# Two settings of a two-block transformer kernel: four on-chip loads moved from ScalarE's queue to SyncE's, and no weight remainders on GpSimd

## The chip, the cores and the metric

One core of a Trainium2 chip. The metric is device time in microseconds of one execution, the median of several runs. TensorE (PE in the profile) multiplies, VectorE (DVE), ScalarE (ACT) and GpSimd (POOL) do the other arithmetic, and SyncE (SP) issues most loads. ACT and POOL can issue loads too: an issue takes its turn in the stream of the engine that makes it.

## What is computed

Two transformer blocks over 256 rows of width 1024, in fp32. The part of the first block that the change touches, cut down:

```python
def compress(kv, pos, w1, b1, w2, b2):
    r = kv.reshape(B, S // 16, 16, G, dk)
    blocks = jnp.concatenate([r[:, :-1], r[:, 1:]], axis=2) + pos
    h = jax.nn.gelu(jnp.einsum('bclgd,ldh->bcgh', blocks, w1) + b1)
    return jnp.einsum('bcgh,hd->bcgd', h, w2) + b2
...
def first_block(x, mem, ...):
    h = rms_norm(x, mix_norm_pre)
    q, kc, vc, ksl, vsl, kw, vw, gt, pin, u, v = jnp.split(h @ w_in, IN_SPLITS, axis=-1)
    out_a = nsa_mixer(...)      # compress(kc), compress(vc), then three softmaxes per head
    out_b = pool_mixer(pin, pool_w, pool_scale)
    out_c = sgu_mixer(u, v, ...)
    x = x + rms_norm(jnp.concatenate([out_a, out_b, out_c], -1) @ w_out, mix_norm_post)
    m = rms_norm(mem, mem_norm_kv)
    x = x + rms_norm(memory_attention(rms_norm(x, mem_norm_pre), m, w_mq, w_mk, w_mv, w_mo), mem_norm_post)
    return x + rms_norm(conv_ffn(rms_norm(x, ffn_norm_pre), ...), ffn_norm_post)
```

The second block follows (a gated delta rule, a sparse attention and a convolution side by side, a second memory attention, an MLP); the change does not touch its settings.

## The kernel before

**Products in three parts.** Each fp32 product is made of three matmuls of a reduced-precision form (`mm3`, L233 to L235): high part by high part, high part by low part and low part by high part. So each weight tile must be split when it arrives. `load_w` (L203 to L224) does this for a tile of 128 x 1024 (or 560) numbers: SP issues its load into `wr` (L208), ACT copies the rounded high part into `wh` (L221), and the DVE subtracts it to get the low part `wl`, in two halves (L223). `wr`, `wh` and `wl` have four buffers each, so a load waits until the weight four before it has been split, and a split until the matmuls of the weight four before it have run.

**Splits on POOL.** A share of the tiles is split in the other way: a counter `due` grows by `share` with each tile, and when it reaches 1 the tile goes through `split` with GpSimd, which makes the whole low part in one instruction (L229), with ACT's copy recorded at L228. `build` sets the share by stage through `give`: `G1` for the mixers of block 1, `GM` for its memory attention, and zero for all that follows. With the settings of before, seven tiles go to POOL: the third `w_in_a` tile and one of `w_out` under `G1`, five in the memory attention under `GM` (two of them of the second memory's key weight, loaded ahead into `bq` and its neighbours). A tile whose `wr` is the second memory's weight appears in the trace with the low part named `bq` or `gd_rhs`.

**Stages.** `block1_mix` makes the products of `w_in` by column chunks (`chunk_T`, 24 matmuls a tile, into `tp`), then those of `w_in_a` (values and gates, into `cc`), and then weaves two streams: `nsa` (the attention) and `fill1` (the two other mixers and, for the memory attention, the memory's norm, `w_mk` and `w_mv` products, into `fl`). After `w_out` come `residual` (norm of the result, added to x) and `block1_mem`.

**The compression.** The compressed keys and values are made in `a0` (named `a`, written by the DVE at L587) and shifted on the chip into `x2`, the second half of the buffer `qT`: for each of two groups one copy as it is (L592) and one shifted by a row into the other 64 partitions (L593). These four are loads from SBUF to SBUF, 128 KB each, and `T['xq']` names the engine that issues them. POOL adds the positions (`cmp_x`, L656, two halves for keys and two for values, in one buffer); TensorE multiplies by `cmp_w1` (L664, loads at L570); a short chain of DVE and ACT steps makes `hid` (gelu); then come L672, L681, and the first scores at L698. POOL also issues the bias table's loads into `bq` (L488) and computes the factor of every norm of rows (`rms_y`, L289) from `rms_v` (DVE, L287).

**Order.** The program is written stage by stage, but a scheduler places the instructions of each engine, by its own estimates, in one order, and each engine runs its own in that order. A change of two settings therefore moves many rows.

The lines on which the change bears:

```python
        for g in range(2):
            getattr(nc, T['xq']).dma_start(x2[0:64, :, g, :], kvc[g * 64:(g + 1) * 64, :, :])
            getattr(nc, T['xq']).dma_start(x2[64:128, :, g, :S - 1], kvc[g * 64:(g + 1) * 64, :, 1:])
...
        self.give(G1)
        x = self.block1_mix()
...
        self.give(GM)
        x = self.block1_mem(x)
```

Of the kernel before, what the change touches and what calls it, by code (L numbers as in the profile page):

```python
# [15 lines left out]
PSUM = bass.MemoryType.PSUM  # L16

FW0 = 1
R1, R2, DS, CV, CK, CV0, NW, FW, WARM, WARM2, G1, GM, GF, G2, GX, GP = 2.0, 2.5, 3, 0.5, 1, 0.25, 24, 14, 7, 4, 0.05, 0.2, 0, 0, 0, 0
T = dict(bp=0, bq='gpsimd', xq='scalar', cp=3, w=(2,3,7,8), n=32, hold=1)  # L20
P = 128
SCRATCH = 4096
S = 256
# [94 lines left out]
class Net:  # L118
# [348 lines left out]
    def build_bias(self):  # L467
# [11 lines left out]

        n, L = T['n'], 8 * 383 + 1  # L480
        copies = self.dp.tile([(n + 1) * L], F32, tag="tz", name="tz")
        rows = copies.rearrange("(p q) -> p q", q=L)[:n, :L - 1].rearrange("p (h u) -> h p u", h=8)
        getattr(nc, T['bq']).dma_start(rows, v[0:8, :383].unsqueeze(1).to_broadcast([8, n, 383]))
        self.biasB = self.t([P, 8, S], "bq8", bufs=1)
        for a in range(P // n):
            o = P - 1 - n * a
            diag = copies[o:o + n * (L - 1)].rearrange("(p q) -> p q", q=L - 1)
            getattr(nc, T['bq']).dma_start(self.biasB[a * n:(a + 1) * n], diag.rearrange("p (h u) -> p h u", u=383)[:, :, :S])  # L488

# [71 lines left out]
    def block1_mix(self):  # L561
# [6 lines left out]
        w1 = self.t([P, 4, 1024], "t3", bufs=1)  # L568
        tasks = [(T['bp'], self.build_bias), (T['cp'], self.more_constants)]
        tasks += [(T['w'][q], lambda q=q: nc.sync.dma_start(w1[:, q], self.i["cmp_w1"][q // 2, q % 2])) for q in range(4)]  # L570

# [19 lines left out]
# [3 lines that stand above are left out]
# [1214 lines left out]
```

## Time and profile before

| | |
|---|---|
| median of 3 runs | 873.55 us (872.27 to 873.56) |
| the profiled execution's own time | 878.08 us |
| its span | 876.3 us, 14992 instructions |
| mean granted TensorE clock | 0.98 of full speed |
| TensorE busy | 842.9 us (96% of the span) |
| VectorE busy | 615.7 us (70%) |
| ScalarE busy | 459.9 us (52%) |
| GpSimd busy | 88.9 us (10%) |
| HBM | 136 MB read, 157 GB/s over the span |

The span is the time from the first to the last instruction of one execution; the execution's own time holds what lies around it, 1.8 us. The profiled execution was 4.5 us longer than the median of the runs without a profile. "Idle before" in a row is the time for which its engine had nothing running just ahead of it, with the instruction that let it go on.

### The profile page before, as it was taken

The numbers are of one execution on the slowest core, as the hardware profiler recorded it, in microseconds if no ns is written. First come the engines' busy times: TensorE is split into PE (matmuls) and PEld (weight loads), VectorE is DVE, ScalarE is ACT, GpSimd is POOL, SyncE is SP. The second block draws the span as 40 slices with busy tenths as digits, with TensorE's granted clock in tenths as the row PEclk, the third lists the DMA queues.
The fourth block names the chain that finished last, engine by engine and source line by source line (L and its number), as shares of the span: only waits on it lengthen the run. The fifth ranks groups of instructions, "written<-read, shape, count | busy, mean of one in ns | idle before, by whom it ended". The sixth has DMA issues, their size and how long they took to land.

```text
span 876.3 us, 14992 instructions
## 1 busy us (share of the span) xinstructions
PE 842.9 (96%) x5725; PEld 768.1 (88%) x5725; DVE 615.7 (70%) x1333; ACT 459.9 (52%) x795; POOL 88.9 (10%) x119
## 2 busy tenths in 40 slices
PE   8899999998999999999999999899899999999998
PEld 6898977878887999999997998879898999999996
DVE  5568765555557878876776797989677776666663
ACT  5246454555655666655555764556456544444442
POOL 1224101121110000000001002520100000000000
PEclk9979999999999999999999998999999999999999
DMA  8985323477343666665652652201163366666661
GB/s 258 293 267 167 98 76 100 149 230 234 128 130 135 208 206 212 218 202 184 190 147 73 197 188 73 82 15 48 50 178 112 97 208 184 188 189 190 182 188 67
DMA packets 41012, 138.94 MB, mean 159 GB/s; under 512 B 4851, under 2 KB 6292, under 8 KB 40940
## 3 DMA queue, kind: packets, MB, share of 16 engines
q1 hardware_dynamic: 37440, 130.49, 47.7%
q10 hardware_dynamic: 2988, 6.06, 2.1%
q0 software_dynamic: 512, 1.44, 1.0%
q8 instruction: 45, 0.74, 0.3%
q14 instruction: 27, 0.22, 0.1%
HBM read 136.00 MB, written 1.44 MB: 157 GB/s over the span
## 4 chain that ended last, share of the span: by engine, by line
PE 79%; DVE 10%; DMA 4%; ACT 3%; issue 2%; POOL 2%; ACTq 0%; SPq 0%; POOLq 0%; DVEq 0%
PE tp L235 10%; PE tp L233 10%; PE tp L234 10%; PE fl L233 6%; PE fl L234 6%; PE fl L235 6%; PE cc L235 5%; PE cc L234 5%; PE cc L233 5%; DVE wl L223 2%; PE cc L751 1%; DVE cv_y L1522 1%; DMA srow<-in_srows_dram 1%; PE tp L729 1%; PE tp L919 1%
## 5 line engine op out<-in xcount | busy, mean ns | idle before, releaser
L223 DVE TENSOR_TENSOR wl<-wr,wh 128x512 fp32r<-128x512 f32 (+2 forms) x448 | 301.3, 698 | 118.7 <-ACT wh L221 116.7
L221 ACT ACTIVATE wh<-wr 128x1024 fp32r<-128x1024 f32 (+2 forms) x224 | 233.0, 1044 | 214.3 <-PE tp L234 80.7
L233 PE MATMUL tp<-thi,wh 128*128 128x256 f32 x784 | 222.7, 284 | 2.0 <-ACT wh L221 2.0
L235 PE MATMUL tp<-thi,wl 128*128 128x256 f32 x784 | 222.7, 284 | 0.2 <-DVE wl L223 0.2
L234 PE MATMUL tp<-tlo,wh 128*128 128x256 f32 x784 | 222.4, 284 | 0.0
L233 PEld LDWEIGHTS tp<-thi,wh 128*128 128x128 f32 x784 | 150.5, 192 | 3.6 <-ACT wh L221 2.2
L234 PEld LDWEIGHTS tp<-tlo,wh 128*128 128x128 f32 x784 | 150.5, 192 | 1.3
L235 PEld LDWEIGHTS tp<-thi,wl 128*128 128x128 f32 x784 | 150.5, 192 | 0.4 <-DVE wl L223 0.4
L228 ACT ACTIVATE ff_h<-ff_y 128x256 fp32r<-128x256 f32 x54 | 22.2, 416 | 42.9 <-PE fl L235 42.0
L233 PE MATMUL fl<-thi,wh 128*128 128x256 f32 x144 | 42.8, 297 | 1.5 <-ACT wh L221 1.4
L235 PE MATMUL cc<-wh,ff_h 128*128 128x512 f32 x108 | 42.4, 393 | 0.0
L973 DVE SCALAR_TENSOR_TENSOR ff_y<-tp,col,ff_y 128x255 f32<-128x255 f32 x88 | 41.9, 476 | 0.7 <-ACT ff_y L971 0.6
L233 PE MATMUL cc<-wh,ff_h 128*128 128x512 f32 x108 | 42.4, 392 | 0.0
L234 PE MATMUL cc<-wl,ff_h 128*128 128x512 f32 x108 | 42.2, 391 | 0.0
L234 PE MATMUL fl<-wl,ff_h 128*128 128x512 f32 x108 | 42.2, 391 | 0.0
L234 PE MATMUL fl<-tlo,wh 128*128 128x256 f32 x144 | 42.1, 292 | 0.0
L233 PE MATMUL fl<-wh,ff_h 128*128 128x512 f32 x108 | 42.1, 390 | 0.0
L235 PE MATMUL fl<-wh,ff_h 128*128 128x512 f32 x108 | 42.1, 391 | 0.0
L235 PE MATMUL fl<-thi,wl 128*128 128x256 f32 x144 | 42.0, 291 | 0.0
L289 POOL TENSOR_TENSOR rms_y<-rms_v,mhalf 128x1 f32<-128x1 f32 x16 | 9.8, 614 | 268.4 <-DVE rms_v L287 268.4
L229 DVE TENSOR_TENSOR ff_h<-ff_y,ff_h 128x256 fp32r<-128x256 f32 x54 | 22.5, 422 | 14.5 <-ACT ff_h L228 14.4
L233 PEld LDWEIGHTS fl<-thi,wh 128*128 128x128 f32 x144 | 28.4, 197 | 2.1 <-ACT wh L221 1.6
(495 smaller groups left out, 1763.2 us busy)
## 6 DMA issues: line engine op xcount, KB each, us to landing
wr<-in_mlp_w_dram SPq DMA_DIRECT2D x64, 512.0 KB, 3.6
wr<-in_w_up_dram SPq DMA_DIRECT2D x44, 512.0 KB, 3.6
wr<-in_w_in_dram SPq DMA_DIRECT2D x31, 512.0 KB, 4.6
wr<-in_w_down_dram SPq DMA_DIRECT2D x22, 512.0 KB, 3.6
wr<-in_w_out_dram SPq DMA_DIRECT2D x16, 512.0 KB, 3.6
grow<-in_rows_dram ACTq DMA_DIRECT2D x8, 512.0 KB, 5.3
wr<-in_w_mk_dram SPq DMA_DIRECT2D x8, 512.0 KB, 4.3
wr<-in_w_mv_dram SPq DMA_DIRECT2D x8, 512.0 KB, 3.5
```

The costliest lines, as they stand in the source:

```text
L221: nc.scalar.activation(hi, raw, AF.Copy)
L223: nc.vector.tensor_tensor(lo[:, q], raw[:, q], hi[:, q].bitcast(F32), op=ALU.subtract)
L228: nc.scalar.activation(hi, raw, AF.Copy)
L229: (eng or nc.vector).tensor_tensor(lo, raw, hi.bitcast(F32), op=ALU.subtract)
L233: nc.tensor.matmul(out, a[0], b[0], start=first, stop=False)
L234: nc.tensor.matmul(out, a[0], b[1], start=False, stop=False)
L235: nc.tensor.matmul(out, a[1], b[0], start=False, stop=last)
L289: self.nc.gpsimd.tensor_tensor(y, v, self.mhalf[:, :1], op=ALU.pow)
L729: nc.tensor.matmul(pc[:, :2 * ns], qT[:, j, tsl], kT[:, :, br, :ns], start=True, stop=True)
L751: nc.tensor.matmul(out[:, h * 64:(h + 1) * 64], pT[:, (e * (i + 1) + b) * P:(e * (i + 1) + b + 1) * P], vsw[b][:, vo:vo + 64], start=(b == ...
L919: nc.tensor.matmul(pc[:, o:o + P], v[b][:, c * P:(c + 1) * P], pT[:, (2 * e + b) * P:(2 * e + b + 1) * P], start=(b == 0), stop=(b == 1))
L973: nc.vector.scalar_tensor_tensor(y[:, e, k:], a[:, :S - k], self.c("conv_w", 44 * (2 - k) + c), y[:, e, k:], op0=ALU.mult, op1=ALU.add)
```

## The change

Two lines of settings:

```diff
-R1, R2, DS, CV, CK, CV0, NW, FW, WARM, WARM2, G1, GM, GF, G2, GX, GP = 2.0, 2.5, 3, 0.5, 1, 0.25, 24, 14, 7, 4, 0.05, 0.2, 0, 0, 0, 0
-T = dict(bp=0, bq='gpsimd', xq='scalar', cp=3, w=(2,3,7,8), n=32, hold=1)
+R1, R2, DS, CV, CK, CV0, NW, FW, WARM, WARM2, G1, GM, GF, G2, GX, GP = 2.0, 2.5, 3, 0.5, 1, 0.25, 24, 14, 7, 4, 0, 0, 0, 0, 0, 0
+T = dict(bp=0, bq='gpsimd', xq='sync', cp=3, w=(2,3,7,8), n=32, hold=1)
```

`xq='sync'` makes SP issue L592 and L593. `G1 = GM = 0` sends all seven tiles through the other branch of `load_w`: ACT's copy at L221 and two DVE halves at L223 instead of one POOL instruction.

On SP, around the loads of the compression (the difference; `wr` are weights, `t` is `cmp_w1`, `a` the source and `qT` the target of the four loads):

```order
 L208 DMA wr_421<-in_w_in_dram 128x1024
 L208 DMA wr_452<-in_w_in_dram 128x1024
+L592 DMA qT_344<-a_54_342 64x2x256
+L593 DMA qT_344<-a_54_342 64x2x255
+L592 DMA qT_344<-a_54_342 64x2x256
+L593 DMA qT_344<-a_54_342 64x2x255
 L208 DMA wr_490<-in_w_in_a_dram 128x560
 L208 DMA wr_509<-in_w_in_a_dram 128x560
-L570 DMA t_36_247<-in_cmp_w_dram 128x1024 x2
 L208 DMA wr_528<-in_w_in_a_dram 128x560
```

The four loads now stand behind two `w_in` weights and ahead of the first two `w_in_a` tiles; two `cmp_w1` loads moved further down.

On POOL, in the compression, before (`wl_531` is the low part of the third `w_in_a` tile; `cmp_x_581` and `cmp_x_675` are the keys' and the values' inputs):

```order
L656 TENSOR_TENSOR cmp_x_581<-qT_344,col 128x512
L488 DMA bq_40_259<-tz 32x8x256 x4
L229 TENSOR_TENSOR wl_531<-wr_528,wh_530 128x560
L656 TENSOR_TENSOR cmp_x_581<-qT_344,col 128x512
...
L656 TENSOR_TENSOR cmp_x_675<-qT_344,col 128x512 x2
L850 TENSOR_TENSOR wsT_767<-wsT_767,con 128x512
L289 TENSOR_TENSOR rms_y_969<-rms_v_967,mhalf 128x1
```

The same place on POOL now:

```order
L656 TENSOR_TENSOR cmp_x_582<-qT_344,col 128x512
L488 DMA bq_40_259<-tz 32x8x256 x4
L656 TENSOR_TENSOR cmp_x_582<-qT_344,col 128x512
...
L289 TENSOR_TENSOR rms_y_970<-rms_v_968,mhalf 128x1
L275 MEMSET rms_ss_1925 128x1
...
L656 TENSOR_TENSOR cmp_x_676<-qT_344,col 128x512 x2
```

The split is gone, and the factor of the memory's first norm (`rms_y_969`, now `rms_y_970`) has moved from behind the values' `cmp_x` pair to ahead of it. On TensorE the `L664` products of that pair stood ahead of the 48 products of `w_in_b`, and now stand behind them and behind ten of the next chunk (`fl_840`), some 58 matmuls later.

On the DVE, at the end of the attention, before (`oa` is the sum of the attention's three branches, `tlo` the low part of its transpose):

```order
L744 COPY pT_1664<-tp_1650 128x512
L765 TENSOR_TENSOR oat_1674<-cc_1517,cf_1670 128x512
L767 TENSOR_TENSOR oa_1291<-oa_1291,oat_1674 128x512
L302 TENSOR_TENSOR tlo_246<-tp_1677,thi_245 128x4x128
L223 TENSOR_TENSOR wl_1789<-wr_1786,wh_1788 128x512 x2
```

The same place on the DVE now:

```order
L744 COPY pT_1665<-tp_1651 128x512
L223 TENSOR_TENSOR wl_1772<-wr_1769,wh_1771 128x512
L765 TENSOR_TENSOR oat_1675<-cc_1518,cf_1671 128x512
L223 TENSOR_TENSOR wl_1772<-wr_1769,wh_1771 128x512
L767 TENSOR_TENSOR oa_1292<-oa_1292,oat_1675 128x512
L223 TENSOR_TENSOR wl_1791<-wr_1788,wh_1790 128x512 x2
L302 TENSOR_TENSOR tlo_246<-tp_1678,thi_245 128x4x128
```

The two halves of the split that POOL made stand on either side of L765, and two halves of the next weight ahead of L302.

## Rows read from the trace of the kernel before

**Rows 1.** The page: parts 1 (engines) and 5 (one group).

```profile
PE 842.9 (96%) x5725; PEld 768.1 (88%) x5725; DVE 615.7 (70%) x1333; ACT 459.9 (52%) x795; POOL 88.9 (10%) x119
...
L223 DVE TENSOR_TENSOR wl<-wr,wh 128x512 fp32r<-128x512 f32 (+2 forms) x448 | 301.3, 698 | 118.7 <-ACT wh L221 116.7
```

**Rows 2.** Busy time by stretch; PEclk, DMA share, GB/s last.

```profile
30.00:35.00 5.00, 3.14 (x14) 2.94 (x15) 3.38 (x7) 3.12 (x4) 0.00 (x0) 0.70 1.08 319
...
45.00:50.00 5.00, 5.00 (x27) 5.00 (x27) 1.82 (x3) 1.06 (x1) 0.03 (x1) 0.57 1.01 231
```

**Rows 3.** Timeline of PE: start, length, line, xcount, [idle before].

```profile
31.64 0.39 PE L233 MATMUL tp<-thi,wh 128*128 128x256 f32 x1 [1.96 <-ACT wh L221]
...
44.25 0.38 PE L233 MATMUL fl<-thi,wh 128*128 128x256 f32 x1 [1.41 <-ACT wh L221]
```

**Rows 4.** Timeline of ACT, 12 to 48 us (ACTq: DMA issues).

```profile
27.74 0.71 ACTq L592 DMA_DIRECT2D qT<-a  x1
...
30.53 3.12 ACT L221 ACTIVATE wh<-wr 128x1024 fp32r<-128x1024 f32 x4 [3.54 <-issue]
```

**Rows 5.** Timeline of SP, 20 to 60 us (SPq: DMA issues).

```profile
22.90 1.90 SPq L208 DMA_DIRECT2D wr<-in_w_in_dram  x2
```

**Rows 6.** Issues in 22.85:24, 27.7:30.5, 35.8:36.3, 61.5:62: KB, us to landing.

```profile
wr<-in_w_in_dram SPq DMA_DIRECT2D x1, 512.0 KB, 6.5
...
qT<-a ACTq DMA_DIRECT2D x2, 127.5 KB, 7.6
...
wr<-in_w_in_dram SPq DMA_DIRECT2D x1, 512.0 KB, 6.8
...
wr<-in_w_mk_dram SPq DMA_DIRECT2D x1, 512.0 KB, 4.7
```

**Rows 7.** The chain that ended last, 0 to 130 us: single steps.

```profile
27.02 0.69 DVE a L587
...
34.87 0.21 PE tp L233
...
37.09 0.12 PE tp L234
```

**Rows 8.** Timeline of POOL, 0 to 70 us.

```profile
37.79 1.14 POOL L656 TENSOR_TENSOR cmp_x<-qT,col 128x512 f32<-128x512 f32 x1 [22.04 <-DMA wr<-in_w_in_a_dram]
...
38.88 2.33 POOL L488 DMA_DIRECT2D bq<-tz  x4
...
66.24 0.58 POOL L289 TENSOR_TENSOR rms_y<-rms_v,mhalf 128x1 f32<-128x1 f32 x1 [8.57 <-DVE rms_v L287]
```

**Rows 9.** Timeline of PE, 52 to 74 us: the compression.

```profile
59.62 4.02 PE L664 MATMUL tp<-cmp_x,t 128*128 128x30 f32 x32
...
70.48 0.30 PE L672 MATMUL tp<-hid,w 128*128 128x30 f32 x2
...
71.91 1.03 PE L698 MATMUL tp<-kcT,qT 128*128 128x32 f32 x8
```

**Rows 10.** Timeline of POOL, 130 to 300 us.

```profile
142.36 2.38 POOL L229 TENSOR_TENSOR wl<-wr,wh 128x1024 fp32r<-128x1024 f32 x1 [3.06 <-issue]
...
173.57 3.07 POOL L229 TENSOR_TENSOR wl<-wr,wh 128x1024 fp32r<-128x1024 f32 x1 [3.00 <-ACT wh L228]
...
207.17 2.41 POOL L229 TENSOR_TENSOR bq<-wr,t 128x1024 fp32r<-128x1024 f32 x1 [2.01 <-ACT t L228]
```

**Rows 11.** Timeline of DVE, 138 to 180 us.

```profile
143.55 1.73 DVE L767 TENSOR_TENSOR oa<-oa,oat 128x512 f32<-128x512 f32 x1
...
175.17 0.15 DVE L287 TENSOR_REDUCE rms_v<-rms_ss 128x1 f32<-128x3 f32 x1
```

**Rows 12.** Timeline of PE, three of its waits.

```profile
145.43 0.63 PE L311 MATMUL tp<-con,oa 128*128 128x128 f32 x4 [0.96 <-DVE oa L767]
...
181.35 0.66 PE L311 MATMUL tp<-con,xh 128*128 128x128 f32 x4 [1.94 <-DVE xh L334]
...
220.03 3.96 PE L937 MATMUL tp<-memk,big 128*128 128x256 f32 x10 [4.20 <-ACT big L932]
```

## Prediction, on record before the changed kernel was run

> **What bounds the kernel now.** I read the page first: TensorE is busy 96% of the span, the DVE 70%, POOL 10% [rows 1]. So time can come only from the few places where TensorE waits or runs at its lower clock; the reader should look for those in the change's stages, not at the busy shares. Then the stretches: from 30 to 50 us the DMA engines are full (share 1.08 and 1.01) and TensorE's granted clock is 0.70 and 0.57 of full speed [rows 2]. Then TensorE's own rows: in that stage it waits twice for the high parts of a weight, 1.96 us until 31.64 and 1.41 us until 44.25 [rows 3]. Outside it, three waits stand near splits that the change takes off POOL: 0.96 us at 145.43, 1.94 us at 181.35, 4.20 us at 220.03 [rows 12]. All of this is under 12 us of 873.55.
>
> **Four loads from ScalarE to SyncE.** ACT's four x2 issues run from 27.74; only then, at 30.53, does its copy of the high parts begin, and that row gives "issue" as the reason for its idle time [rows 4]. The weight it copies was issued at 22.90 [rows 5] and took 6.5 us [rows 6]: there at 29.4. TensorE ran out of work at 31.64 − 1.96 = 29.68.
>
> Term a: with ACT free the copy starts at 29.4 instead of 30.53, 1.1 us sooner, and the wait falls from 1.96 to 0.87. I take −1.1. Bounds: 0 (the second weight behind it comes late as before) and −1.96.
>
> Term b: after that wait a single matmul takes 0.21 us, later 0.12 [rows 7]: the lower of the two clock levels, 1.2 against 2.4 GHz. The trace has waits of about 1 us after which the clock stayed, the one at 145.43 among them, and the one of 1.96 after which it fell. A wait of 0.87 should leave it up: 12 matmuls × 0.09 = −1.1; the bounds are that and 0.
>
> SyncE takes the issues instead. Their source is ready at 27.02 + 0.69 = 27.71 [rows 7], so ACT was not late with its first one at 27.74, and SP cannot be sooner. In SP's order they stand behind two weight loads (22.90 to 24.8 [rows 5]) and ahead of the first two w_in_a tiles, which had gone out while `a` was still being made. So SP now idles to 27.7, issues the four for 2.7 us as ACT did (0.71 and less each [rows 4]), and the two tiles and a cmp_w1 load go out after 30.4. Two things follow. The x2 transfers find the DMA engines emptier: they took 7.6 us [rows 6]; I take half of that for the last, so POOL, which waited for them to 37.79, starts some 3.6 us sooner, and with it the bias loads bq that it issues from 38.88 [rows 8]. And w_in_a comes later: a 512 KB load took 4.7 us where the engines were less full and 6.5 to 6.8 in this stage [rows 6], so it lands between 35.1 and 37.2. TensorE has 48 products of the two weights at hand, from about 30.5 at 0.12 [rows 7], which is 36.3. I cost this at nothing; that work hides it, and if the cover is gone it is up to 1.9 us (37.2 + 1.0 for copy and low part, less 36.3), which stands in the range.
>
> Term c: the wait at 44.25 is for a weight that was issued within 35.8 to 36.3 and took 6.8 us [rows 6], landing at 42.7. The bq loads now go 3.6 us sooner and take their share beside it; I give half of that to its delay: 44.6 with the rest of a microsecond for SP's later turn. Its copy takes about 1.0 (four in a row, two of them of half width, took 3.12 [rows 4]): 45.7. TensorE was there at 44.25 − 1.41 = 42.84; it is 2.2 us ahead, at 40.6, but the order now puts 22 products of w_in_a (0.13 each, 2.9) and half a compression stream (1 to 2 us, by rows 9 a stretch of 32 in 4.02) before it: 45.0. The wait falls from 1.41 to 0.7: −0.7. Bounds −1.41 and +2.3 (the load at about 48).
>
> Here a rule speaks against the change. The rows show that ACT's time is freed; they do not show that any transfer lands sooner. The Trainium skill, "DMA: Bandwidth & Descriptors", section "Issuing engines are not separate DMA queues", says that loads run on the same 16 DMA engines whoever starts them, and that another issuer saves the sequencer's time alone. The trace agrees in the full share of 1.08. By the rule taken strictly only a and b would stand; that is the first rival.
>
> Term d: from 45.7 to 52.5 the clock is at its lower level (0.57 in the stretch from 45 to 50) [rows 2]. It follows the 1.41 wait. 22 matmuls of the w_in_a product would run there, of 280 columns, so 0.23 against 0.13 by the pitches 0.21 and 0.12 for 256: −2.2. With even chances a new, shorter fall comes (14 × 0.09 = 1.3, half of it 0.65): −1.55. Bounds −2.2 and 0.
>
> Term e, a loss: the order puts the end of the compression later, with less work between its steps. cmp_x has one buffer; POOL needs 1.14 us for a half [rows 8], TensorE has 6 matmuls, 0.7 us, between: +0.45. From L672 to L698 took 71.91 − 70.48 = 1.43 us [rows 9]; now 5 matmuls (0.6) cover it: +0.8. From there to L681 I allow another 0.5. Together +1.8. Bounds 0 (other work covers it) and the price of the second rival.
>
> **No low parts on POOL.** Seven splits leave POOL: 1.40 to 3.07 us each there. A wide one becomes two DVE instructions of 0.70 us [rows 1]: 6 × 1.4 + 0.8 = 9.2 us more on the DVE, which is busy 615.7 us and has 30% of the span free. Where the DVE is ahead of TensorE this costs nothing; what hides it is a split that is done some tiles before its use. If that cover is gone, up to 9.2.
>
> Term f: the w_out split on POOL runs from 142.36 for 2.38 us [rows 10]; beside it the DVE's L767 takes 1.73 us [rows 11] where a 128x512 step takes 0.70 [rows 1], and TensorE waits 0.96 us for it [rows 12]. With POOL silent it loses 1.0 us, while one half of the split now stands between L765 and L767 (+0.7) and five matmuls (0.6) are put into the gap. I take −0.9; bounds −0.96 and +0.3.
>
> Term g: POOL computes the norm's rms_y. Its input is there at 175.17 + 0.15 = 175.32, but POOL is in a split from 173.57 to 176.64 [rows 10, 11]: 1.3 us late. The wait at 181.35 hangs on this norm. Half a split on the DVE stands ahead of the xh step, 0.7: net −0.6, and half a chance that the fall of the clock at 182 goes with the shorter wait, −0.7. Together −1.3; bounds −2.0 and +0.7.
>
> Term h: the same pattern at 207.17, where POOL is in a split for 2.41 us and the norm follows. The wait of 4.20 at 220.03 ends with work behind that norm [rows 10, 12]. I take −0.9, between 0 and −1.7, since other loads lie between.
>
> Term i: in the memory attention's softmax the split halves now stand between the DVE's short steps: two halves of 0.70 on a chain that TensorE waits for, less what lies beside other work: +1.0; bounds 0 and +2.1.
>
> Sum: −1.1 − 1.1 − 0.7 − 1.55 + 1.8 − 0.9 − 1.3 − 0.9 + 1.0 = −4.75. By the profiled execution's own time that is 878.08 − 4.75 = 873.3; it stands 4.5 us (0.5%) above the median of the runs, 873.55, so the prediction is the median less 4.75: 868.8.
>
> **Rivals.** A, no change: the loads are bound by the full DMA engines, and the earlier bq pushes the weight of term c to about 48 us. Then c is +2.3 and d is 0; the sum is −4.75 + 3.0 + 1.55 = −0.2, 873.4. For it: share 1.08 in the stage. Against it: the x2 loads take their 0.5 MB out of the stage sooner, and the total to be moved is the same. Chance 0.20.
>
> B, slower: one mechanism on POOL. In the new order the memory's rms_y stands ahead of the second pair of cmp_x steps, and ACT's copy of the first w_mk weight stands ahead of the square that this norm needs. TensorE's second compression stream began at 59.62 [rows 9]; it now stands some 58 matmuls later in its order (7 us), less the 4 us won, so about 62.5. If the memory's loads come as before, the first w_mk (issued about 61.6, 4.7 us [rows 6]) lands at 66.3; then copy 1.06, square 0.8, the norm 0.15 + 0.58, cmp_x 1.14 [rows 4, 8]: 70.0. TensorE waits 7.5 us and a fall of the clock adds 1.3. In place of e: −4.75 − 1.8 + 8.8 = +2.25, 875.8. It decides if that load lands after 59 us (62.5 less the 3.7 of that chain). For it: before, the norm's rms_y came at 66.24 [rows 8]. Against it: TensorE leaves the w_in_a weights 3 to 5 us sooner, so their buffers, and the loads behind them, come sooner too. Chance 0.17.
>
> C, better: e is covered, both new falls of the clock stay away, i is hidden: −4.75 − 1.8 − 0.65 − 0.7 − 1.0 = −8.9, 864.65. Chance 0.15.
>
> That the change does not do what it says can be left out: the orders show the issues on SP and no split on POOL.
>
> **How the numbers follow.** The forecast has 0.48, A 0.20, B 0.17, C 0.15. Under 0.2% (1.75 us) a measurement of this kernel cannot tell a time from no change. Faster takes the forecast, C and a sliver of A: 0.64; same is the rest of A: 0.19; slower is B: 0.17. The range reaches from C, less its own 0.6, to A and the milder part of B: 864.0 to 874.5. The forecast's own range is 866.5 to 871.5.
>
> **What would show it.** Right: in the profile after, ACT's copy near 29.4 with no "issue" idle, no lower clock from 32 to 35, a wait under 1 us near 45, L767 at 0.7 us, rms_y within 0.3 us of its rms_v. Wrong: a wait of several microseconds of TensorE for POOL's cmp_x between 60 and 70 us (B); the weight after the w_in_a product landing at 47 or later with a low clock behind it (A); waits for wl with the DVE as the one that ends them in the memory attention, beyond 2 us in all (then i was too small).

## The result, and the profile after

The changed kernel took 882.8 us (median of 4 runs, 881.87 to 885.95) against 873.31 us of the kernel before beside it: 1.0107 times as long, 95% interval 1.0076 to 1.0139. That is 9.5 us **slower**, where 4.75 us faster had been forecast. Its profiled execution took 881.97 us, near its own median; the one of before was 4.5 us above its median, so the two traces differ by less (3.9 us of span) than the medians. The clock tells why: TensorE's mean granted clock was 0.980 in that execution of before, and its median is 0.986 (0.981 to 0.990) in the runs of the same kernel beside the experiments. An estimate from this: 0.006 of 876 us, so the trace of before has some 5 us more of lost clock than a usual run.

The page of the changed kernel, parts 1 and 5:

```profile
PE 843.7 (96%) x5725; PEld 768.6 (87%) x5725; DVE 620.7 (71%) x1347; ACT 461.0 (52%) x795; POOL 73.8 (8%) x112
...
L223 DVE TENSOR_TENSOR wl<-wr,wh 128x512 fp32r<-128x512 f32 (+2 forms) x460 | 307.9, 695 | 133.5 <-ACT wh L221 131.7
```

Against [rows 1] POOL has lost 15 us of work, the DVE has gained 5, and TensorE's share is the same 96%: the page hides the loss. The stretches show it (same columns as [rows 2]):

```profile
30.00:35.00 5.00, 5.00 (x42) 5.00 (x43) 2.84 (x6) 2.17 (x3) 1.53 (x2) 1.00 1.04 311
...
45.00:50.00 5.00, 2.77 (x11) 2.55 (x12) 1.41 (x3) 2.27 (x3) 0.00 (x0) 0.61 0.99 294
60.00:65.00 5.00, 2.32 (x19) 2.12 (x18) 1.95 (x5) 3.38 (x8) 0.68 (x4) 1.00 0.29 100
65.00:70.00 5.00, 5.00 (x32) 4.82 (x31) 3.62 (x18) 0.71 (x4) 2.81 (x5) 0.66 0.94 314
70.00:75.00 5.00, 5.00 (x26) 5.00 (x25) 0.60 (x4) 0.82 (x1) 1.04 (x1) 0.50 0.00 0
75.00:80.00 5.00, 5.00 (x25) 5.00 (x25) 3.96 (x14) 1.59 (x4) 3.20 (x4) 0.50 0.06 25
```

From 30 to 35 us the loss of before is gone (clock 1.00, TensorE busy throughout). From 45 to 50 nothing is won: TensorE works 2.77 us, and the clock is still low. From 60 to 65 TensorE works 2.32 of 5 us, and from 70 to 80 it is busy all the time at the lower of its two levels, 0.50. TensorE's timeline tells what it does there:

```profile
29.25 0.39 PE L233 MATMUL tp<-thi,wh 128*128 128x256 f32 x1 [0.15 <-ACT wh L221]
...
42.09 1.87 PE L664 MATMUL tp<-cmp_x,t 128*128 128x30 f32 x16
47.23 0.58 PE L233 MATMUL fl<-thi,wh 128*128 128x256 f32 x1 [3.27 <-ACT wh L221]
...
64.43 0.38 PE L233 MATMUL fl<-thi,wh 128*128 128x256 f32 x1 [2.68 <-ACT sg_v L857]
...
68.33 7.03 PE L664 MATMUL tp<-cmp_x,t 128*128 128x30 f32 x32
...
79.59 1.29 PE L698 MATMUL tp<-kcT,qT 128*128 128x32 f32 x8
...
188.69 1.32 PE L311 MATMUL tp<-con,xh 128*128 128x128 f32 x8 [1.05 <-DVE xh L334]
...
225.59 4.97 PE L937 MATMUL tp<-memk,big 128*128 128x256 f32 x14 [3.82 <-ACT big L932]
```

The waits of [rows 3] went from 1.96 to 0.15 us and from 1.41 to 3.27 us; a new one of 2.68 us stands at 64.43. The values' stream of L664, which took 4.02 us for 32 records in [rows 9], takes 7.03. (A record is one row of the trace; each L664 instruction leaves two.) The transposition that began at 181.35 in [rows 12] begins at 188.69, 7.3 us later. By then TensorE has waited 3.1 us more in all (14.2 against 11.0), and has had 20.5 us at the lower level (6.8 from 46.1, 13.7 from 66.6) against 13.7 us before; half of the 6.8 us between them is lost: 3.4 us. Over the whole span the two traces have the same time at the lower level (35 us), since before has falls behind 181 us that are not there now. In the runs of the changed kernel the mean granted clock is 0.982, against the 0.986 of before; on 880 us the 0.004 is 3.5 of the 9.5 us. The rest would be waiting, of which the traces show 3.0 us; the other 3 us are not shown.

What TensorE waits for at 64.43 is the evacuation of the w_in_b products (`sg_v`, L857), which must leave the accumulator banks `fl` before the next products can go into them. ScalarE, timeline:

```profile
58.26 0.63 ACT L837 ACTIVATE sg_u<-sg_u 128x512 f32<-128x512 f32 x1
...
61.59 1.06 ACT L221 ACTIVATE wh<-wr 128x1024 fp32r<-128x1024 f32 x1 [2.09 <-DMA wr<-in_w_mk_dram]
...
63.92 0.46 ACT L857 ACTIVATE sg_v<-fl,rt 128x256 f32<-128x256 f32 x1
64.06 0.35 ACTq L818 DMA_DIRECT2D pl_c<-in_invcnt_dram  x1
64.28 0.46 ACT L857 ACTIVATE sg_v<-fl,rt 128x256 f32<-128x256 f32 x1
```

The copy of the first `w_mk` weight at 61.59 waited 2.09 us for its load; two squares follow, and only then comes `sg_v`, though its products were done at 61.75. GpSimd, timeline, and the wait's other side, the DMA issues of 28.4 to 28.6 and 35.4 to 35.6:

```profile
33.47 1.14 POOL L656 TENSOR_TENSOR cmp_x<-qT,col 128x512 f32<-128x512 f32 x1 [19.17 <-DMA qT<-a]
34.55 2.32 POOL L488 DMA_DIRECT2D bq<-tz  x4
...
64.12 0.57 POOL L289 TENSOR_TENSOR rms_y<-rms_v,mhalf 128x1 f32<-128x1 f32 x1 [24.32 <-DVE rms_v L287]
...
67.15 2.20 POOL L656 TENSOR_TENSOR cmp_x<-qT,col 128x512 f32<-128x512 f32 x2 [2.34 <-PE tp L664]
```

```profile
qT<-a SPq DMA_DIRECT2D x1, 127.5 KB, 4.8
...
wr<-in_w_in_dram SPq DMA_DIRECT2D x1, 512.0 KB, 10.6
```

The x2 loads land in 4.8 us instead of 7.6 [rows 6] and POOL starts 4.3 us earlier than at 37.79 [rows 8], bq too (1.3 of the 4.3 because the first x2 load goes out at 26.44 and not at 27.74); the weight that TensorE waits for to 47.23 now takes 10.6 us instead of 6.8.

### The profile page after: what moved, and what is told of

It reads as the page before. It is cut to its first block, busy times and chain, and to the rows that moved or that the text cites. A ratio compares the mean times of both kernels' runs of the same rounds, so it can differ in the third digit from the quotient of the medians.

```text
span 880.2 us, 15013 instructions
## 1 busy us (share of the span) xinstructions
PE 843.7 (96%) x5725; PEld 768.6 (87%) x5725; DVE 620.7 (71%) x1347; ACT 461.0 (52%) x795; POOL 73.8 (8%) x112
## 3 DMA queue, kind: packets, MB, share of 16 engines
q0 software_dynamic: 512, 1.44, 0.9%
HBM read 136.00 MB, written 1.44 MB: 156 GB/s over the span
## 5 line engine op out<-in xcount | busy, mean ns | idle before, releaser
L223 DVE TENSOR_TENSOR wl<-wr,wh 128x512 fp32r<-128x512 f32 (+2 forms) x460 | 307.9, 695 | 133.5 <-ACT wh L221 131.7
L221 ACT ACTIVATE wh<-wr 128x1024 fp32r<-128x1024 f32 (+2 forms) x230 | 239.4, 1043 | 226.5 <-PE tp L234 79.1
L234 PE MATMUL fl<-tlo,wh 128*128 128x256 f32 x144 | 44.2, 307 | 0.0
L235 PE MATMUL fl<-thi,wl 128*128 128x256 f32 x144 | 43.9, 305 | 0.0
L235 PE MATMUL cc<-wh,ff_h 128*128 128x512 f32 x108 | 42.4, 393 | 0.0
L233 PE MATMUL cc<-wh,ff_h 128*128 128x512 f32 x108 | 42.4, 392 | 0.0
L233 PEld LDWEIGHTS fl<-thi,wh 128*128 128x128 f32 x144 | 30.3, 211 | 6.5 <-ACT wh L221 3.4
```

What stands on the lines that cost most here:

```text
L221: nc.scalar.activation(hi, raw, AF.Copy)
L223: nc.vector.tensor_tensor(lo[:, q], raw[:, q], hi[:, q].bitcast(F32), op=ALU.subtract)
L233: nc.tensor.matmul(out, a[0], b[0], start=first, stop=False)
L234: nc.tensor.matmul(out, a[0], b[1], start=False, stop=False)
L235: nc.tensor.matmul(out, a[1], b[0], start=False, stop=last)
```

## The experiments

Theory: the loss is the late place of the compression. L664 comes in three runs (16 records for the first half of the keys, 16 for the second, 32 for the values). Before, 22 and 46 other products stood between them; now 100 and 6, so that the last 48 records come late and close together. Rivals: the DVE's 14 more halves cost as such, or SyncE's issues do. Times are medians, ratios are to the kernel before run beside. Where an edit adds lines, the lines behind it have numbers a little higher (L664 is L665 to L668 there).

**One part at a time.**

```diff
-xq='scalar'
+xq='sync'          (e1)
-G1, GM = 0.05, 0.2
+G1, GM = 0, 0.2    (e2)
+G1, GM = 0.05, 0   (e3)
```

> Only the four x2 loads go to SyncE; the shares G1 and GM stay 0.05 and 0.2. In the built order both compression streams (L664) again stand behind the w_in_b products and inside the next chunk, as in the changed kernel. Theory (late compression order is the loss): 879 to 885 us, with a lower-clock stretch of 7 us or more around the L664 products after 60 us. Rival 1 (the DVE's 14 extra halves are the loss): 872 to 874, since they are not here. Rival 2 (SyncE's issues and the earlier bq push the weight loads): 879 or more, with the loss before 50 us.

> Only G1 is 0; the x2 loads stay on ScalarE, GM stays 0.2. Two splits less on GpSimd, in the first block's mixers. In the built order the second half of the keys' stream and the values' stream stand behind w_in_b. Theory (late compression order): 879 to 885 us. Rival 1 (DVE halves): 874 to 876, two sevenths of the loss. Rival 2 (SyncE's issues): 872 to 874, since SyncE issues what it did.

> Only GM is 0; the order of the first 100 us is that of before. Theory (late compression order): 871 to 873.5 us, no loss, perhaps 1 to 2 us won where rms_y no longer stands behind a split on GpSimd. Rival 1 (DVE halves are the loss): 879 to 881, five sevenths of the loss. Rival 2: 873.

> The run with GM = 0 alone once more, with more rounds, beside the two above: 870 to 872 us, 0.1 to 0.5% under the kernel before.

e1: 887.67 us, 1.0176 (1.0146 to 1.0206). e2: 883.71 us, 1.0134 (1.0115 to 1.0154). e3: 871.26 us, 0.9970 (0.9944 to 0.9995), and in its second series 870.91 us, 0.9970 (0.9948 to 0.9992). So xq alone costs more than the whole change, G1 alone cannot be told from it (the intervals overlap), and the third part, GM, is a gain of 0.3%. That fits the theory: e1 and e2 both build the late place, e3 the early one; e1 is slower than the theory's 879 to 885. In e2 the DVE has only two splits more, in e3 five; the rival of the DVE's halves is out. In e2 SyncE issues what it did, so its issues are not needed for the loss either. e1's trace by stretch:

```profile
60.00:65.00 5.00, 5.00 (x45) 5.00 (x44) 1.44 (x3) 2.40 (x5) 0.00 (x0) 0.99 0.58 190
65.00:70.00 5.00, 4.77 (x32) 4.48 (x31) 3.87 (x12) 0.00 (x0) 3.17 (x3) 0.70 0.69 234
70.00:75.00 5.00, 5.00 (x25) 5.00 (x25) 0.25 (x3) 1.79 (x4) 0.08 (x1) 0.50 0.00 0
```

and its TensorE timeline there:

```profile
63.03 3.66 PE L664 MATMUL tp<-cmp_x,t 128*128 128x30 f32 x32
...
68.01 7.03 PE L664 MATMUL tp<-cmp_x,t 128*128 128x30 f32 x32 [0.23 <-POOL cmp_x L656]
```

Here no wait over 0.25 us comes between 56.7 and 84: the clock falls at 67.0, between the two L664 runs, while TensorE is busy, and stays down for 13.7 us. In e2 TensorE waits 5.89 us until 58.24 for the evacuation of the chunk before (`sg_u`, L836), and runs the last 32 records in 6.10 us:

```profile
58.24 0.58 PE L233 MATMUL fl<-wh,thi 128*128 128x256 f32 x1 [5.89 <-DVE sg_u L836]
```

**The place itself.** e5 keeps both edits and restores the early place; e6 keeps neither and makes it late; e7 puts the keys' stream early, the values' late; e8 is e5 with the x2 loads on ScalarE.

```diff
+with self.tc.high_priority(2000):                      (e5, e8; e7: 2000 if s == 0 else 0)
     nc.gpsimd.tensor_tensor(xa[:, half]..., op=ALU.add)     # L656
...
+with self.tc.high_priority(-130 if q and not s else 0):   (e6, on the kernel before)
     nc.tensor.matmul(pc[...], raw[...], rhs, ...)           # L664
```

> Both edits as in the change, and GpSimd's cmp_x steps given precedence over its bias-table issues, which is one line around L656. In the built order TensorE's two compression streams then stand as in the kernel before (right behind w_in_a, and ahead of w_in_b). Theory (the late place of the compression is the loss): the loss goes, 866 to 874 us, and between 55 and 85 us there is no wait over 2 us and no lower-clock stretch over 7 us. Rival (the edits cost as such, by the DVE's 14 more halves or SyncE's issues): 879 to 885.

> Neither edit. The kernel before, with the second half of the keys' L664 products given a later place, so that TensorE's order has them and the values' stream where the changed kernel has them (inside the chunk behind w_in_b). Theory (late place of the compression): as slow as the change, 879 to 886 us, with a lower-clock stretch of 7 us or more over the L664 products after 60 us. Rival (the edits cost as such): 872 to 874.5.

> Both edits, and only the keys' cmp_x steps given precedence over the bias-table issues. In the built order the keys' stream stands right behind w_in_a, the values' stream still behind w_in_b and inside the next chunk. Theory (late place of the compression): between the two, 872 to 880 us, since half of the L664 products and the keys' gelu chain are out of the late place. Rival (the edits as such): 879 to 885.

> G1 = GM = 0 with the x2 loads on ScalarE, and the same precedence of all cmp_x steps. Order of TensorE's compression as before. Theory (late place of the compression): 867 to 874 us, and against the run with both edits and this precedence it tells what the x2 loads on SyncE are worth by themselves: by term a and b of the prediction that one should be 1 to 2 us faster. Rival (DVE halves as such): 879 or more.

e5: 875.61 us, 1.0022 (0.9990 to 1.0054). e6: 883.82 us, 1.0128 (1.0103 to 1.0154). e7: 877.65 us, 1.0064 (1.0041 to 1.0087). e8: 874.12 us, 1.0012 (0.9995 to 1.0029). e6 shows that the late place alone, without the edits, costs the whole loss; in e5 and e8 the edits are there, the place is early, and the loss is gone; e7 lies between, as expected. e5 and e8 missed their expectation a little (up to 874, and e8 is not slower than e5): what the x2 loads win on SyncE cannot be told from nothing. e6 on TensorE:

```profile
59.76 0.58 PE L233 MATMUL fl<-wh,thi 128*128 128x256 f32 x1 [4.31 <-DVE sg_u L837]
...
69.87 5.72 PE L665 MATMUL tp<-cmp_x,t 128*128 128x30 f32 x32 [0.47 <-POOL cmp_x L656]
```

and e5:

```profile
44.80 3.66 PE L665 MATMUL tp<-cmp_x,t 128*128 128x30 f32 x32
...
54.12 3.66 PE L665 MATMUL tp<-cmp_x,t 128*128 128x30 f32 x32
...
65.69 0.38 PE L233 MATMUL fl<-thi,wh 128*128 128x256 f32 x1 [1.94 <-ACT sg_v L858]
```

In e6 the wait for `sg_u` is 4.31 us and the stream takes 5.72. In e5 each stream takes 3.66 us, 5.7 us of other products lie between them, and the clock stays up; but the wait for `sg_v` remains, 1.94 us, and 6.8 us at the lower level follow it. e5's edit also moves the bias loads: one bq goes out at 36.22, three only at 50.78.

```profile
wr<-in_w_in_dram SPq DMA_DIRECT2D x2, 512.0 KB, 7.4
...
50.78 1.73 POOL L488 DMA_DIRECT2D bq<-tz  x3
```

So the weights that took 10.6 us beside four bq loads take 7.4, and the wait near 45 is gone as well. By itself e5 does not separate the two; e6, where no bq load moves ahead, does.

**Wait or clock?** Theory A: the wait for the evacuation costs and brings the low clock. Theory B: a long run of L664 products brings it. e9 frees `sg_v` by holding the memory's load until `sg_u` is made; e10 puts the values' stream 48 records later still; e11 has both streams close together in another place; e16 doubles the products in the kernel before.

```diff
+if name == "mem" and i == 0: self.hold(m, self.behind)   (e9, e12: behind = sg_u)
     nc.sync.dma_start(m, self.i[name][i])                   # L344
...
+with self.tc.high_priority(-200 if s else 0):             (e10, around L664)
...
-G1, GM = 0, 0; xq='sync'
+G1, GM = 0.05, 0; xq='gpsimd'                            (e11)
...
-for q in range(2):
+for q in (0, 1, 0, 1):                                   (e16, on the kernel before)
     raw = w1[:, 2 * s + q]
```

> Both edits, late place of the compression as in the change, but the load of the memory is held until sg_u is made, so that on ScalarE the evacuation of the w_in_b products (sg_v) stands ahead of the memory's squares and of the copy of the first w_mk weight. Theory A (the wait for sg_v behind the w_mk copy is what costs, and it sets off the low clock): the 2.7 us wait is gone and the low clock after 60 us lasts 3.4 us or less, 873 to 877 us. Theory B (the two L664 streams close together bring the low clock themselves): the wait is gone but a low-clock stretch of 7 us or more remains over the L664 products, 877 to 881 us.

> Both edits; the values' L664 stream gets a later place still, so that some 40 products and L673, L699 lie between the two streams; ScalarE's order is as in the change. Theory A (wait for sg_v): the wait of 2 to 3 us stays, 880 to 885 us. Theory B (streams close together): the low clock after 60 us is cut to two stretches of 3.4 us or one of 7, 877 to 881 us.

> GM = 0, G1 = 0.05 as before, the x2 loads issued by GpSimd, which alone waits for them. In the built order both L664 streams stand in the middle of the first fl chunk, six products apart, ahead of w_in_b, and sg_v ahead of the w_mk copy. Theory A (wait for sg_v): 868 to 872 us, a little under the run with GM = 0 alone, since ScalarE's copy of the weight no longer waits behind the x2 issues. Theory B (streams close together): a low-clock stretch of 7 us or more over L664, 873 to 878 us.

> The kernel before, with every L664 product of the compression made twice in a row (the second pass writes the same numbers); TensorE's order is otherwise that of before. By themselves the 64 further records take 7 to 8 us at the higher clock. Theory A (these products leave the clock as it is; the loss is in the waits): 879 to 882 us. Theory B (a long run of them brings the lower clock): a low-clock stretch of 7 us or more over them, 884 to 890 us.

e9: 884.08 us, 1.0118 (1.0085 to 1.0151), above the range of either theory. The wait for `sg_v` is gone, and a stretch of 6.8 us at the lower level begins within L664 all the same (69.0), as B has it; but the held load made the memory late:

```profile
90.28 0.47 PE L742 MATMUL tp<-con,pr 128*128 128x128 f32 x1 [3.72 <-ACT pr L739]
```

It waits 3.72 us there, 1.44 and 1.30 before it, and has 10.2 us more at the lower level. e10: 883.85 us, 1.0112 (1.0072 to 1.0151): the waits stay (2.26, 1.40, 2.15 us). The time is A's number, and B's shorter stretch did not come: 6.8 us at the lower level from 64.8 and 13.7 from 81.9, with new waits of 0.91 us between them, on the gelu chain, and of 1.13 and 1.79 us within the second. The distance is not isolated by this run. e11: 880.73 us, 1.0083 (1.0052 to 1.0114). ScalarE does not block there, but new waits of 4.71 and 4.07 us for weights end at 43.77 and 48.68 us, and the second 32 records of L664 take 6.94 us at the lower level; B's stretch is seen, and both numbers are missed. e16 is the clean one, 888.04 us, 1.0159 (1.0122 to 1.0197): 13.7 us for products that take 7.3 at the higher level. TensorE has no wait over 0.25 us between 42.4 and 91:

```profile
47.30 5.46 PE L664 MATMUL tp<-cmp_x,t 128*128 128x30 f32 x48
...
59.66 10.82 PE L664 MATMUL tp<-cmp_x,t 128*128 128x30 f32 x64
```

```profile
65.00:70.00 5.00, 5.00 (x25) 5.00 (x25) 0.00 (x0) 0.00 (x0) 0.00 (x0) 0.50 0.14 56
```

48 records still go in 5.46 us (0.114 each), with 3.4 us at the lower level behind them; of the 64 in the next run, more than half are at the lower level: 10.82 us, 0.17 each, in a stretch of 10.3 us from 62.8. The kernel before has 3.4 us from 62.7, with 32 records there. So both act: the waits for `fl` banks, and the clock that falls in a long run of L664. How the 9.5 us divide between them is not measured by a run; the traces give an estimate below.

**Both edits without the late place and without the block.**

```diff
+if self.behind is not None: self.hold(raw, self.behind); self.behind = None   (e13, e14: once, at w_mk)
     nc.sync.dma_start(raw, ap)                                               # L208
```

> Both edits, all cmp_x steps given precedence over the bias-table issues (compression early, streams 48 products apart) and the memory's load held until sg_u is made (sg_v not behind the w_mk copy). Theory A and B agree here: the run with the precedence alone had a wait of 1.94 us for sg_v and 6.8 us of low clock behind it; both go, 869 to 873 us. If the memory's products come to wait for their own weights instead, 876 or more.

> Both edits, all cmp_x steps given precedence over the bias-table issues (streams early and 48 products apart), and only the first w_mk load held until sg_u is made, so that on ScalarE sg_v stands ahead of the w_mk copy while the memory's norm keeps its place. If the late place, with the sg_v wait, is all that the two edits cost: 867 to 872 us, under the kernel before and at or under the run with GM = 0 alone. If the edits cost something as such: 873 or more.

> GM = 0 alone with the same hold of the first w_mk load. The run with GM = 0 alone had a wait of 1.14 us for sg_v and 3.4 us of low clock behind it; both go, 868 to 871 us. If the hold makes w_mk late instead, 873 or more.

e12 (e5 with e9's hold): 878.24 us, 1.0054 (1.0032 to 1.0077). TensorE reaches the first attention products at 71.2 us, 10 us ahead of the kernel before, and then waits 3.35 and 2.25 us for the memory's norm: the hold was on the wrong load. e13 (e5, with only the first `w_mk` load held): 870.82 us, 0.9961 (0.9937 to 0.9984): faster than both kernels, with both edits in it. e14 (GM = 0 with that hold): 872.97 us, 0.9980 (0.9960 to 1.0001), a miss, and no better than GM = 0 alone; TensorE waits 2.11 us for `sg_u` there instead. e13 on TensorE:

```profile
42.91 3.74 PE L668 MATMUL tp<-cmp_x,t 128*128 128x30 f32 x32
...
53.74 4.29 PE L668 MATMUL tp<-cmp_x,t 128*128 128x30 f32 x32
...
75.09 0.33 PE L314 MATMUL fl<-con,xh 128*128 128x128 f32 x1 [1.40 <-DVE xh L337]
...
55.00:60.00 5.00, 5.00 (x32) 5.00 (x32) 0.56 (x3) 1.80 (x4) 0.00 (x0) 0.66 0.63 194
```

(The last line is a stretch.) No wait over 0.25 us between 31.1 and 73.7, though 10.2 us at the lower level remain there (46.3 to 49.8 and 56.6 to 63.4, both in or behind a stream). So a run of 32 records can bring a fall too, with 7.1 us of other products ahead of it. e13 and GM = 0 alone cannot be told apart (0.9961 and 0.9970): with the order repaired, xq and G1 neither cost nor win what these runs can measure.

One more way to the early place, bq on SyncE too:

```diff
-bq='gpsimd'
+bq='sync'           (e4, with both edits)
```

> Both edits as in the change, and the five bias-table transfers (tz, bq) issued by SyncE too instead of GpSimd. In the built order the keys' stream then stands right behind the first w_in_a products and the values' stream ahead of w_in_b, as in the kernel before. Theory (late compression order): the loss goes, 868 to 875 us, no lower-clock stretch over 7 us between 60 and 85. Rival 1 (DVE halves): stays at 880 to 884. Rival 2 (SyncE's issues): 882 to 888, since SyncE has five more.

e4: 881.34 us, 1.0098 (1.0066 to 1.0129), a miss. Its compression is early and from 36 to 186 us TensorE has no wait over 0.4 us, but it pays ahead of it, and has 17 us at the lower level (24.9 to 41.9):

```profile
35.78 0.58 PE L233 MATMUL tp<-thi,wh 128*128 128x256 f32 x1 [14.00 <-ACT wh L221]
```

```profile
22.95 0.71 SPq L592 DMA_DIRECT2D qT<-a  x1
...
28.37 1.10 SPq L208 DMA_DIRECT2D wr<-in_w_in_dram  x2
```

SP's order had the x2 loads and bq ahead of the `w_in` weights: SP stood from 13.2 to 22.95 for the source of x2, and the weight went out at 28.37, not at 22.90 [rows 5]. TensorE waited 14 us for it.

## Why the prediction was wrong

- **Term e** is the step that failed and turned the sign. "Together +1.8" counted gaps between dependent steps. Measured, the late place brings a wait of 2.68 us, and 13.7 us at the lower level where before had 3.4, of which half is lost: 2.7 + 5.1 = 7.8 us. Two things were missed: that the L664 runs now follow each other almost without other products between them, where the clock falls and each record takes 0.22 instead of 0.11 us; and who else stands behind the `w_mk` copy on ScalarE. Behind the late compression TensorE also waits 3.2 us between 84 and 92 us, in five waits, where before has one of 0.73.
- **Terms a and b** held: ScalarE's copy came in time (wait 0.15 us, less than the 0.87 forecast) and the fall of the clock at 32 us went. The other traces bear it out with some scatter: with the x2 loads on ScalarE this wait is 1.62 to 3.41 us, and the clock falls with it in four of eight; on SyncE with bq on GpSimd it is 0.11 to 2.11 or none, and the clock falls in one of eight (e5). e8 against e5 shows no gain of it in the whole; later waits may have taken it.
- **SyncE's queue** did as said: idle until the source was there, POOL sooner by 4.3 us (forecast 3.6), no wait of TensorE for w_in_a. A part of that is luck: the source itself was ready sooner, where the prediction had "SP cannot be sooner".
- **Term c** failed. "I give half of that to its delay: 44.6", and TensorE at 45.0. The weight took 10.6 us and landed at 46.0; TensorE was there at 43.96. The wait is 3.27 us where 0.7 was forecast, so +1.9 instead of −0.7, within the bound of +2.3. Rival A's mechanism was right here. The rule of the Trainium skill that the prediction set against the change ("DMA: Bandwidth & Descriptors", section "Issuing engines are not separate DMA queues") is that loads run on the same 16 DMA engines whoever starts them. The trace agrees: what bq won, this weight lost. The runs show it too: beside four bq loads the weight takes 10.2 to 12.1 us (the change, e7, e9, e10), beside one 7.3 and 7.4 (e13, e5).
- **Term d** failed with it: the stretch at the lower level is still 6.8 us long (46.1 to 52.9), 0 instead of −1.55.
- **Rival B** had the right instruction and the wrong victim. It saw the copy of the first `w_mk` weight ahead of the square, and its "decides if that load lands after 59 us" came true (61.5). But it priced the norm and `cmp_x`, which TensorE hardly waited for; the victim was `sg_v`. Its sum, +2.25, is 7 us under the measured 9.5.
- **Term f** held: L767 takes 0.69 us and no wait stands at w_out (−0.96). Every trace with G1 = 0.05 has this wait (0.96 to 0.98 us) and none with G1 = 0.
- **Term g** held in its wait: 1.94 us at 181 is 1.05 (−0.9), and it is 1.94 to 2.01 in all traces with GM = 0.2 and 0.98 to 1.05 in all with GM = 0. That the clock stays up behind it (−1.7, which takes the term past its bound of −2.0) is not shown to come from it: e1, e6 and e16 keep the splits and the wait, and their clock is up there too.
- **Term h** is not shown: 4.20 became 3.82, but over the traces this wait is 3.57 to 4.20 us with GM = 0.2 and 3.68 to 4.53 with GM = 0 (e4 aside). e3 has g and h without the rest of the change: 0.3%, 2.6 us, of which the traces explain the 0.9 of g's wait.

```profile
152.97 0.69 DVE L767 TENSOR_TENSOR oa<-oa,oat 128x512 f32<-128x512 f32 x1
...
187.93 0.66 PE L311 MATMUL tp<-con,xh 128*128 128x128 f32 x4 [1.94 <-DVE xh L334]
...
185.00:195.00 10.00, 7.77 (x42) 5.94 (x41) 8.89 (x17) 5.59 (x11) 1.56 (x4) 1.00 0.74 247
```

(The last two lines are e6's.)

- **Term i** (+1.0) was not seen: from L937, where the memory attention begins, to L1437 in the second block TensorE waits 6.4 us against 6.6.

By the two traces these come to some +2 us, and the waits between 84 and 92 us to 2.5 more, where the spans differ by 3.9. One error lies under several terms: b, d and the half of g that is clock priced falls read from one execution of before, whose clock was lower than in its usual runs (0.980 against 0.986), so a part of what they were to win was probably not there to be won in the median.

What stays open: why the scheduler puts the rest of the compression so late when G1 or xq changes. e5 shows that giving `cmp_x` precedence over the four bq issues on GpSimd is enough to bring the early place back; by which estimate the scheduler chose the late one was not tried. Why the clock stays up over a run of 32 records in some traces and falls in others is open too.

## What to carry to other kernels

A setting that takes two instructions off one engine can make a scheduler rewrite the order of all engines, and the new order can cost far more than the instructions: e2 took two splits off POOL (1.40 and 2.38 us in the trace of before) and lost 1.3%. Read from the order what has moved, and for each engine ask what stands behind its next wait, above all the evacuation of an accumulator that the next product needs. When the order is what costs, pin the place (a precedence, a held load) and judge the edit then: here a version with both edits and the order repaired is 0.4% under the kernel before, and the bare edits are 1.1% over it. Test parts alone: the one part that left the order as it was (GM = 0) was a gain all along, and by itself gives what the repaired version gives. Before pricing a fall of the clock, see whether more than one execution has it.

## What the runs showed of the hardware

The granted clock of TensorE fell not only behind waits but in the middle of unbroken work: in e16 within a run of 64 records of 30 columns, in e1 between two runs of 32 with 1.3 us of other products between them, both followed by stretches where TensorE is busy 5.00 of 5.00 us at 0.50. With 5.7 us of 256-column products between the two runs of 32 it stayed at the higher level in e5; in e13, with 7.1 us between them, it fell in the second. Over the traces: where two L664 runs have 6 or 7 other products between them, or one has 64 records (the change, e1, e2, e6, e9, e11, e16), the clock falls in them or between them every time; where more lies between, it falls in or right behind a run of 32 in some (before, e4, e8, e10, e13, e14) and at no such run in others (e3, e5, e12, e15); in e7 it falls behind a wait of 2.00 us just ahead of one. A load of 512 KB took 10.6 us beside the four bq loads, against 6.8 us when it was issued ahead of them.
